# Gated DeltaNet decays: from triangle products on two engines to differences of running sums, in a two-layer decoder trunk

## The chip, the core and the metric

The kernel runs on one core of a Trainium2 chip. The core has TensorE (PE, with its weight loads PEld), VectorE (DVE), ScalarE (ACT), GpSimd (POOL) and SyncE (SP), which each work through their own instructions in order, and DMA engines that move data between DRAM and the core's memory. The metric is the device time of one execution in microseconds (us). Before the change the median of three runs is 2967.11 us, from 2965.97 to 2969.26.

## The reference

A trunk of two layers over 256 tokens of 2048 features: layer 0 mixes tokens by an mLSTM, layer 1 by a gated DeltaNet; both then attend to 256 memory tokens and apply a squared-ReLU MLP of 8192 features. All in float32. The change lies in the DeltaNet of layer 1 (32 value heads, 16 key heads, head size 128, chunks of 64). What matters of it:

```python
beta = jax.nn.sigmoid(bt)
g = -jnp.exp(a_log) * jax.nn.softplus(a + dt_bias)
gam = jnp.cumsum(to_chunks(g), axis=-1)
diff = gam[..., :, None] - gam[..., None, :]
A   = einsum('...id,...jd->...ij', kb, kc) * exp(where(strict, diff, -inf))   # kb = beta k
Aqk = einsum('...id,...jd->...ij', qc, kc) * exp(where(causal, diff, -inf))
# U, W by triangular solves with I + A; then a scan over the chunks
```

For each head and each pair of tokens j <= i the decay is the exponential of the sum of g over the tokens after j up to i.

## The kernel before, in words

Every product with weights streams units of one MB by SP's DMA queue into `raw`; ACT casts each half to `hi` (L88) and DVE makes the rest `lo` (L89), both rounded to float32r; PE multiplies hi by hi, hi by the input's lo and lo by hi. There are four raw halves and two hi and two lo tiles, so a unit is split while PE works on the one before it. In the DeltaNet's input product most units are tall: all 2048 rows and 128 columns, 48 matmuls of 256 columns, which give one block of 128 features of q (gq), k (gk), v (gv) or the gate (gz).

Each such block goes through `conv`: DVE scales it into a padded tile (`pad`), ACT multiplies it with the first tap (`cv`), DVE adds three taps, ACT applies Silu. POOL clears the pad's first columns.

The program treats all 256 tokens at once rather than chunks of 64: for each group of four value heads the function `pairs` builds blocks of A and of the query's matrix as [j, i] tiles of 128 by 128 tokens, for the token halves (0,0), (1,1) and (0,1). It asks `decays` for `dm` (the decay times beta), multiplies q and k by k on PE into the PSUM tiles g0 and g1 (g in the profile), scales and masks these into `gm` (DVE, and ACT for the third block), multiplies `gm` by `dm` into `at` (DVE, four instructions of 768 columns), and sends `at` to DRAM by POOL's queue (`at_d`, `a_d`), where a later stage reads it. PSUM tiles of the kind `ps` have three banks in turn for everything of that sort.

In `decays` before, POOL multiplies the triangle of ones (j <= i) by each head's g, once for the rounded part `gh` and once for the rest `gl` (L931). PE multiplies these by the opposite triangle, or by ones for the block (0,1), into `gep` (L935, six matmuls of 512 columns for a group), and ACT takes the exponential with ln beta as bias (L939), twelve instructions of 128 columns for a group. `norms` gives 1/norm of k (`rk`, by squares `l2sq` on ACT, sums `l` on PE, a square root on ACT and a reciprocal on DVE), which `gm` needs.

The order in the stage: for c = 0 to 3 four gq units, then `norms` and `pairs` of the group before, four gk units, then the other `pairs`; after c = 0 `gates` makes beta and g. Groups 6 and 7 lie among the first gv units. This is the program's order; the framework's scheduler sets the order on each engine from it, and interleaves neighbouring parts. The tables of ACT's functions are loaded where two neighbouring functions in its final order need different ones.

Of the kernel before, what the change touches and what calls it, by code (L numbers as in the profile page):

```python
# [7 lines left out]
F32 = mybir.dt.float32  # L8
# [6 lines left out]
P = 128  # L15
# [19 lines left out]
class Weights:  # L35
    """Streams weight units [128, kb, n] from DRAM and splits each into hi + lo."""
# [8 lines left out]
    def add(self, key, w, k0, kn, n0, nn, tall=False):  # L45
        """Units of 512 rows and 512 columns or, tall, of all the rows and 128 columns (64 at most: hi and lo side
        by side)."""
# [6 lines left out]
    def begin(self, place=None):  # L54
        """Starts the next unit's loads; returns the two halves' splits, to be called in order.
        place(j) gives other tiles to hold the unit: hi and lo of its j-th 128 rows."""
# [54 lines left out]
def trunk(ctx: ExitStack, tc, x, mem, norm_g, mem_norm_g, w_mem_kv, w_xq, w_xo, w_up, w_down,  # L111
# [56 lines left out]
    # rows j, columns i: j <= i, j < i, j > i  # L168
    tri_le, tri_lt, tri_gt = mask("tri_le", ALU.is_ge, 1), mask("tri_lt", ALU.is_gt, 1), mask("tri_gt", ALU.is_gt, -1)

    def behind(ins, *others):
        """Issue order on an engine: ins after each of the others."""
# [4 lines left out]
    # per-feature vectors as columns [128 features, 128-blocks]  # L177
# [27 lines left out]
    def feed(tok, c, h, gains, then=None):  # L205
        """Features 512 c .. of a token-major tile (t, 512 features): feature-major, gained and split into h."""
# [13 lines left out]
    class Rms:  # L220
        """Sums of squares along the features of token-major tiles [128 tokens, 512] by ACT."""
# [18 lines left out]
    def split_into(dst, src, scale=None):  # L240
        """dst[:, 0:256] = round(scale * src), dst[:, 256:512] = what is left."""
# [14 lines left out]
    def token_sums(parts, name):  # L256
        """Sums over the partitions of the parts' sum, as columns [128 tokens, 2]."""
# [11 lines left out]
    def spread(dst, col0, col1):  # L269
        """dst[p, t] = the token's scalar on every partition."""  # L270
        for t, c in enumerate((col0, col1)):
            PE.matmul(dst[:, t * P : (t + 1) * P], c.to_broadcast([P, P]), ident, start=True, stop=True)

    class Bank:
        """A block of a product: complete in the first 256 columns, or two parts in the two halves (wide)."""
# [4 lines left out]
    def extra_unit(u0):  # L280
        """Prepares one more unit of weights in tiles of u that are free around the end of a sub-layer."""
# [10 lines left out]
    def prod_feat(key, srcs, n_fb, evac, wide=True, before=None, fresh=False):  # L292
        """Feature-major product: srcs[k] = [128, hi 256 | lo 256]; evac(fb, bank).
        fresh: the sources are only being made, each one's hi first."""
# [30 lines left out]
    def prod_tall(key, srcs, n_fb, evac, before=None):  # L325
        """Feature-major product by tall units, one block after the other."""
# [921 lines left out]
```

## Time and profile before

| what | value |
|---|---|
| median of three runs | 2967.11 us |
| span of the profiled execution | 2962.9 us |
| PE busy in it | 2912.0 us (98%) |
| DVE, ACT, POOL busy | 1762.6, 1449.7, 137.1 us |
| mean granted PE clock | 0.996 |
| stage with the decays | 1313 to 1560 us, 247 us |
| PE, DVE, ACT, POOL busy in the stage | 233.6, 178.9, 154.1, 80.2 us |

The span runs from the first to the last instruction of the profiled execution; the time of that execution outside the span is not shown, and the median of the runs lies 4.2 us above it. The page names an engine's instructions by line, tile written and tiles read, with count, busy time and mean length, and with what its engine waited for just before. A wait belongs to whatever ended it last. PE's matmuls overlap, so a single duration is longer than the time a matmul adds to a full queue; the count in a stretch of full work gives the latter. Rows with a window give busy times in a stretch, in us from the span's start.

### The profile page before, as it was taken

The numbers are of one execution on the slowest core, as the hardware profiler recorded it, in microseconds if no ns is written. First come the engines' busy times: TensorE is split into PE (matmuls) and PEld (weight loads), VectorE is DVE, ScalarE is ACT, GpSimd is POOL, SyncE is SP. The second block draws the span as 40 slices with busy tenths as digits, with TensorE's granted clock in tenths as the row PEclk, the third lists the DMA queues.
The fourth block names the chain that finished last, engine by engine and source line by source line (L and its number), as shares of the span: only waits on it lengthen the run. The fifth ranks groups of instructions, "written<-read, shape, count | busy, mean of one in ns | idle before, by whom it ended". The sixth has DMA issues, their size and how long they took to land.

```text
span 2962.9 us, 43790 instructions
## 1 busy us (share of the span) xinstructions
PE 2912.0 (98%) x17363; PEld 2545.9 (86%) x17363; DVE 1762.6 (59%) x2560; ACT 1449.7 (49%) x2245; POOL 137.1 (5%) x256
## 2 busy tenths in 40 slices
PE   8999999999999999999999999999999999999998
PEld 7888888988888888898889998899888888888887
DVE  5555657644545555677779745445567546455565
ACT  6454546544434344566655444444456444344343
POOL 0000000000000000013231111000000000000000
PEclk9999999999999999999999999999999999999999
DMA  7545565555555565556778955665445565565554
GB/s 237 175 154 164 190 197 163 171 195 186 189 194 185 195 189 189 180 143 188 198 210 223 268 168 176 209 183 165 163 150 184 186 196 183 193 191 189 189 191 168
DMA packets 423120, 553.27 MB, mean 187 GB/s; under 512 B 22769, under 2 KB 220914, under 8 KB 420610
## 3 DMA queue, kind: packets, MB, share of 16 engines
q1 hardware_dynamic: 412608, 507.12, 55.5%
q0 software_dynamic: 8736, 42.02, 4.3%
q8 instruction: 136, 2.23, 0.3%
q10 hardware_dynamic: 1570, 1.33, 0.1%
q14 instruction: 70, 0.57, 0.1%
HBM read 527.29 MB, written 23.10 MB: 186 GB/s over the span
## 4 chain that ended last, share of the span: by engine, by line
PE 92%; DMA 3%; DVE 3%; ACT 2%; issue 1%; DVEq 0%; ACTq 0%; SPq 0%
PE up L314 15%; PE up L315 8%; PE down L378 8%; PE down L380 8%; PE down L379 8%; DMA raw<-in_gdn_w_in 3%; PE gz L334 2%; PE gz L335 2%; PE gz L333 2%; PE g_out L378 2%; PE g_out L379 2%; PE g_out L380 2%; PE o L314 2%; PE gv L333 1%; PE gv L334 1%; PE gv L335 1%
## 5 line engine op out<-in xcount | busy, mean ns | idle before, releaser
L89 DVE TENSOR_TENSOR lo<-raw,hi 128x1024 fp32r<-128x1024 f32 x938 | 1122.8, 1224 | 888.0 <-ACT hi L88 886.6
L88 ACT CAST hi<-raw 128x1024 fp32r<-128x1024 f32 x938 | 950.4, 1046 | 980.8 <-PE down L380 310.8
L314 PE MATMUL up<-h,hi 128*128 128x512 f32 x1920 | 678.7, 399 | 0.0
L315 PE MATMUL up<-h,lo 128*128 128x256 f32 x1920 | 539.2, 281 | 0.0
L314 PEld LDWEIGHTS up<-h,hi 128*128 128x128 f32 x1920 | 360.8, 188 | 89.9
L379 PE MATMUL down<-lo,u 128*128 128x512 f32 x1024 | 398.4, 389 | 0.0
L378 PE MATMUL down<-hi,u 128*128 128x512 f32 x1024 | 398.4, 389 | 0.0
L380 PE MATMUL down<-hi,u 128*128 128x512 f32 x1024 | 398.3, 389 | 0.0
L315 PEld LDWEIGHTS up<-h,lo 128*128 128x128 f32 x1920 | 362.7, 189 | 0.2
L380 PEld LDWEIGHTS down<-hi,u 128*128 128x128 f32 x1024 | 192.2, 188 | 40.0
L378 PEld LDWEIGHTS down<-hi,u 128*128 128x128 f32 x1024 | 192.2, 188 | 40.0
L379 PEld LDWEIGHTS down<-lo,u 128*128 128x128 f32 x1024 | 192.2, 188 | 39.7
L334 PE MATMUL gz<-h,hi 128*128 128x256 f32 x512 | 151.2, 295 | 0.0
L333 PE MATMUL gz<-h,hi 128*128 128x256 f32 x512 | 146.5, 286 | 2.5 <-ACT hi L88 2.5
L335 PE MATMUL gz<-h,lo 128*128 128x256 f32 x512 | 146.1, 285 | 0.8 <-DVE lo L89 0.8
L333 PE MATMUL gv<-h,hi 128*128 128x256 f32 x512 | 145.9, 285 | 0.5 <-ACT hi L88 0.5
L335 PE MATMUL gv<-h,lo 128*128 128x256 f32 x512 | 145.4, 284 | 0.0
L334 PE MATMUL gv<-h,hi 128*128 128x256 f32 x512 | 145.2, 284 | 0.0
L334 PEld LDWEIGHTS gz<-h,hi 128*128 128x128 f32 x512 | 97.8, 191 | 6.2 <-issue 6.2
L378 PE MATMUL g_out<-hi,u 128*128 128x512 f32 x256 | 100.9, 394 | 0.0
L379 PE MATMUL g_out<-lo,u 128*128 128x512 f32 x256 | 100.7, 393 | 0.0
L333 PEld LDWEIGHTS gz<-h,hi 128*128 128x128 f32 x512 | 97.9, 191 | 3.1 <-ACT hi L88 2.7
(415 smaller groups left out, 4889.0 us busy)
## 6 DMA issues: line engine op xcount, KB each, us to landing
raw<-in_w_up SPq DMA_DIRECT2D x256, 512.0 KB, 3.9
raw<-in_w_down SPq DMA_DIRECT2D x256, 512.0 KB, 4.0
raw<-in_gdn_w_in SPq DMA_DIRECT2D x192, 512.0 KB, 5.0
raw<-in_mlstm_w_in SPq DMA_DIRECT2D x96, 512.0 KB, 4.0
raw<-in_gdn_w_out SPq DMA_DIRECT2D x64, 512.0 KB, 4.4
raw<-in_mlstm_w_out SPq DMA_DIRECT2D x32, 512.0 KB, 4.5
at_d<-at POOLq DMA_DIRECT2D x8, 1536.0 KB, 7.6
ab<-at_d POOLq DMA_DIRECT2D x8, 1536.0 KB, 7.6
```

The lines of the kernel that those rows point to most:

```text
L88: a = nc.scalar.copy(h_, raw[:, :, :n])
L89: return a, nc.vector.tensor_tensor(l_, raw[:, :, :n], h_, ALU.subtract)
L314: PE.matmul(a[:fw], wh, srcs[kk][:, :], start=(kk == 0), stop=False, skip_group_check=True)
L315: PE.matmul(a[:fw, T:], wl, srcs[kk][:, 0:T], start=False, stop=(kk == nk - 1), skip_group_check=True)
L333: PE.matmul(a[:, 0:T], hi[k], srcs[k][:, 0:T], start=(k == 0), stop=False)
L334: PE.matmul(a[:, 0:T], hi[k], srcs[k][:, T:], start=False, stop=False)
L335: m = PE.matmul(a[:, 0:T], lo[k], srcs[k][:, 0:T], start=False, stop=(k == nk - 1))
L378: PE.matmul(accs[t], sh, hi[j], start=(kk == 0), stop=False)
L379: PE.matmul(accs[t], sh, lo[j], start=False, stop=False)
L380: PE.matmul(accs[t], sl, hi[j], start=False, stop=(kk == nk - 1))
```

## The change

`gates` makes the running sums of g within each half of 128 tokens instead of the two rounded parts: `cum` as columns (a token for each partition, a head for each column) and, by the same product the other way round, `cumr` as rows (a head for each partition). The rows go to DRAM (`g_d`). `load_rows` reads four heads' rows back by POOL's queue, the same 512 values to every partition (`grow`), two loads for a group; groups 0 and 1 are loaded after `gates`, each further one at the end of `decays` two groups ahead. `decays` subtracts the column's value as a scalar from the row and limits the difference to at most zero (`gdiff`, DVE, two buffers that share the tag of the norms' gains), and ACT takes the exponential with the same biases as before. The block (0,1) needs no difference: its bias is the sum over the rest of the first half, so ACT reads `grow` itself. There are 96 exponentials as before. Neither `gep` nor POOL's products remain. Comments were also removed, and line numbers shift by 1 to 14.

```diff
@@ gates
-                gh = sc.tile([P, 2, 32], F32R, name="gh")
-                V.tensor_copy(gh, g)
-                gl = sc.tile([P, 2, 32], F32R, name="gl")
-                V.tensor_tensor(gl, g, gh, ALU.subtract)
                 p_ = psum("suf")
                 PE.matmul(p_[:, 0:32], tri_gt, g[:, 0, :], start=True, stop=True)
+                for t in range(2):
+                    PE.matmul(p_[:, 32 + t * 32 : 64 + t * 32], tri_le, g[:, t, :], start=True, stop=True)
+                    PE.matmul(p_[0:32, P + t * P : 2 * P + t * P], g[:, t, :], tri_le, start=True, stop=True)
                 sufb = sc.tile([P, 32], F32, name="sufb")
                 V.tensor_tensor(sufb, p_[:, 0:32], lnb[:, 0, :], ALU.add)
-                return lnb, gh, gl, sufb
+                cum = sc.tile([P, 2, 32], F32, name="cum")
+                V.tensor_copy(cum, p_[:, 32:96].rearrange("p (t h) -> p t h", t=2))
+                cumr = sc.tile([32, 2 * P], F32, name="cumr")
+                V.tensor_copy(cumr, p_[0:32, P : 3 * P])
+                nc.gpsimd.dma_start(g_d, cumr)
+                return lnb, cum, sufb
+
+            rows_of = {}
+
+            def load_rows(grp):
+                rows_of[grp] = []
+                for tt in range(2):
+                    r_ = acts.tile([P, 4, P], F32, tag=f"u{8 + grp % 2 * 2 + tt}", name="grow")
+                    src = g_d[grp * 4 : grp * 4 + 4, tt * P : (tt + 1) * P]
+                    nc.gpsimd.dma_start(r_, src.unsqueeze(0).to_broadcast([P, 4, P]))
+                    rows_of[grp].append(r_)
 
             def decays(grp):
                 dm = [acts.tile([P, 2, 3, P], F32, tag=f"y{grp % 2 * 2 + i}", name="gdm") for i in range(2)]
-                for blk, tt, lhs in ((0, 0, tri_gt_r), (1, 1, tri_gt_r), (2, 1, ones_r)):
-                    ep = psum("gep")
-                    if blk < 2:
-                        rr = []
-                        for i, src in enumerate((gh, gl)):
-                            r_ = acts.tile([P, 4, P], F32R, tag=f"u{8 + 2 * tt + i}", name=f"gl{tt}{i}")
-                            G.tensor_tensor(r_, tri_le[:, None, :].to_broadcast([P, 4, P]),
-                                            src[:, tt, grp * 4 : grp * 4 + 4].unsqueeze(2).to_broadcast([P, 4, P]), ALU.mult)
-                            rr.append(r_)
-                    for i in range(2):
-                        PE.matmul(ep, lhs, rr[i].rearrange("p h i -> p (h i)"), start=(i == 0), stop=(i == 1))
-                    for hh in range(4):
-                        hv = grp * 4 + hh
-                        b_ = sufb[:, hv : hv + 1] if blk == 2 else lnb[:, tt, hv : hv + 1]
-                        S.activation(dm[hh // 2][:, hh % 2, blk, :], ep[:, hh * P : (hh + 1) * P], AF.Exp, bias=b_)
+                gr = rows_of.pop(grp)
+                for hh in range(4):
+                    hv = grp * 4 + hh
+                    d = tmp.tile([P, 2, P], F32, tag="gain", name="gdiff")
+                    for tt in range(2):
+                        V.tensor_scalar(d[:, tt, :], gr[tt][:, hh, :], cum[:, tt, hv : hv + 1], 0.0,
+                                        ALU.subtract, ALU.min)
+                    o_ = dm[hh // 2][:, hh % 2]
+                    for tt in range(2):
+                        S.activation(o_[:, tt, :], d[:, tt, :], AF.Exp, bias=lnb[:, tt, hv : hv + 1])
+                    S.activation(o_[:, 2, :], gr[1][:, hh, :], AF.Exp, bias=sufb[:, hv : hv + 1])
+                if grp + 2 < GV_H // 4:
+                    load_rows(grp + 2)
                 return dm
@@ the loop over c
-                    lnb, gh, gl, sufb = gates()
+                    lnb, cum, sufb = gates()
+                    load_rows(0)
+                    load_rows(1)
```

The scheduler gives other orders on three engines. First ACT, in the gq units of c = 2 (rows are line, instruction, tile written and tile read; hi is a cast, cv a convolution's first tap, gqk its Silu). Before:

```order
L88 CAST hi_11815<-raw_0_11817 128x1024
L88 CAST hi_11815<-raw_8_11819 128x1024
L868 ACTIVATE cv<-pad,cols 128x256
L88 CAST hi_11883<-raw_0_11885 128x1024
L871 ACTIVATE gqk_11743<-cv 128x256
L868 ACTIVATE cv<-pad,cols 128x256
L88 CAST hi_11883<-raw_8_11887 128x1024
L871 ACTIVATE gqk_11744<-cv 128x256
```

And in the change, at the same place:

```order
L88 CAST hi_11891<-raw_0_11893 128x1024
L88 CAST hi_11891<-raw_8_11895 128x1024
L948 ACT_TABLE_LOAD
L948 ACTIVATE gdm<-gdiff,lnb 128x128
L872 ACT_TABLE_LOAD
L872 ACTIVATE gqk_11752<-cv 128x256
L869 ACTIVATE cv<-pad,cols 128x256
L88 CAST hi_11959<-raw_0_11961 128x1024
L88 CAST hi_11959<-raw_8_11963 128x1024
```

One exponential of a later group now stands between the cast and the Silu, with a table load on either side; before, a group's exponentials stood together.

Second PE, at the first pairs: in the change the end of the first gk unit of c = 1 (gk_11425) and what follows; g_11395 and g_11396 are of group 0, the other g of group 1, gk_11493 the next unit.

```order
L335 MATMUL gk_11425<-h_10290,lo_11254 128x256
L993 MATMUL g_11395<-gqk_10425 128x512
L994 MATMUL g_11396<-gqk_10425 128x256
L993 MATMUL g_11719<-gqk_10426 128x512
L994 MATMUL g_11720<-gqk_10426 128x256
L993 MATMUL g_11731<-gqk_10427 128x512
L333 MATMUL gk_11493<-h_10275,hi_11415 128x256
L334 MATMUL gk_11493<-h_10275,hi_11415 128x256
L333 MATMUL gk_11561<-h_10275,hi_11483 128x256
L334 MATMUL gk_11561<-h_10275,hi_11483 128x256
L335 MATMUL gk_11493<-h_10275,lo_11416 128x256
```

Before, the next unit followed the first at once, with gep and g singly among its matmuls; now five g stand in a row ahead of it.

Third DVE, at the end of group 3, before the weights `lo_12462` of the unit gq_12539, the second gq unit of c = 3 (gk_12335 is the last gk unit of c = 2, gq_12471 the first gq unit of c = 3). Before:

```order
L992 TENSOR_TENSOR at<-gm,gdm 128x6x128
L870 SCALAR_TENSOR_TENSOR cv<-pad,cols,cv 128x256
L984 SCALAR_TENSOR_TENSOR gm<-g_12431,rk,tri_lt 128x128
L986 SCALAR_TENSOR_TENSOR gm<-g_12432,rk,tri_lt 128x128
L984 SCALAR_TENSOR_TENSOR gm<-g_12431,rk,tri_le 128x128
L986 SCALAR_TENSOR_TENSOR gm<-g_12432,rk,tri_le 128x128
L89 TENSOR_TENSOR lo_12456<-raw_8_12459,hi_12455 128x1024
L992 TENSOR_TENSOR at<-gm,gdm 128x6x128 x2
L865 TENSOR_TENSOR pad<-gq_12465,rb 128x256
L89 TENSOR_TENSOR lo_12524<-raw_0_12525,hi_12523 128x1024
```

And in the change:

```order
L998 SCALAR_TENSOR_TENSOR gm<-g_12438,rk,tri_lt 128x128
L871 SCALAR_TENSOR_TENSOR cv<-pad,cols,cv 128x256
L998 SCALAR_TENSOR_TENSOR gm<-g_12438,rk,tri_le 128x128
L871 SCALAR_TENSOR_TENSOR cv<-pad,cols,cv 128x256 x2
L944 TENSOR_SCALAR gdiff<-grow,cum 128x128 x4
L1004 TENSOR_TENSOR at<-gm,gdm 128x6x128 x4
L89 TENSOR_TENSOR lo_12462<-raw_0_12463,hi_12461 128x1024
L89 TENSOR_TENSOR lo_12462<-raw_8_12465,hi_12461 128x1024
```

The four at stood in smaller pieces with a lo among them; now they stand together, ahead of both halves of the lo.

More of the change, by code (lines that the diff above doesn't have):

```diff
@@ L855, in gdn @@
         v_d = tc.dram_tile([GV_H // 4, P, 2, 512], F32, name="v_d")
+        g_d = tc.dram_tile([32, 2 * P], F32, name="g_d")
         rs = Scales(rms.rstd, "gd")
@@ L889, in gdn @@
         with tc.tile_pool(name="gd1", bufs=1) as sc:
-            tri_gt_r = sc.tile([P, P], F32R, name="tri_gt_r")
-            V.tensor_copy(tri_gt_r, tri_gt)
-            ones_r = sc.tile([P, P], F32R, name="ones_r")
-            V.tensor_copy(ones_r, ones)
             dtb = sc.tile([P, 32], F32, name="dtb")
```

## The prediction

> **What bounds the kernel now.** I read the page's busy shares and its chain first, then the tables by stretch for the stage that the change touches, then what TensorE (PE) waits for there.
>
> ```profile
> span 2962.9 us, 43790 instructions
> PE 2912.0 (98%) x17363; PEld 2545.9 (86%) x17363; DVE 1762.6 (59%) x2560; ACT 1449.7 (49%) x2245; POOL 137.1 (5%) x256
> PE 92%; DMA 3%; DVE 3%; ACT 2%; issue 1%; DVEq 0%; ACTq 0%; SPq 0%
> ```
>
> PE is busy 98% of the span and holds 92% of the chain, so a matmul taken away is worth its slot, unless PE then waits. The runs' median is 2967.11, 4.2 us above this span; I make the sum on the span and carry the 4.2.
>
> ```profile
> core 0: us, PE busy (x) PEld busy (x) DVE busy (x) ACT busy (x) POOL busy (x), PEclk, DMA share, GB/s
> 1160.00:1180.00 20.00, 20.00 (x90) 16.57 (x89) 11.94 (x12) 9.06 (x13) 0.00 (x0) 1.00 0.60 197
> 1240.00:1260.00 20.00, 20.00 (x171) 20.00 (x170) 15.03 (x25) 14.74 (x31) 0.00 (x0) 1.00 0.53 142
> 1320.00:1340.00 20.00, 17.45 (x112) 14.20 (x111) 12.86 (x21) 16.46 (x36) 10.05 (x11) 1.00 0.18 59
> ...
> 1377.00:1441.00 64.00, 60.84 (x446) 56.45 (x445) 45.78 (x75) 39.28 (x70) 20.14 (x34) 0.97 0.67 184
> ...
> 1313.00:1560.00 247.00, 233.62 (x1735) 216.66 (x1734) 178.94 (x295) 154.09 (x276) 80.21 (x138) 0.99 0.69 190
> ```
>
> The last row is the stage with the decays: 247 us, in which PE sits idle 13.4. The first two rows give the slots of a full PE, which the single durations (400 and 283 ns, overlapping) do not: 20/90 = 0.222 us for a matmul of 512 columns, 20/171 = 0.117 for one of 256. A weight unit of 48 is thus 5.6 us. The row 1377 to 1441 is one c, four gq and four gk units: PE 60.8 us, ACT 39.3.
>
> ```profile
> PE gk L335 <- DVE lo L89: 5.2, 6, 1.2
> ...
> PEld gk L335 <- DVE lo L89: 9.0, 6, 2.0
> ```
>
> In that stage PE waits mostly for weights not yet split (lo by VectorE, DVE, after hi by ScalarE, ACT). So whatever delays a hi or lo there is paid by PE.
>
> **What goes.** 48 matmuls on gep, and their operands made by POOL.
>
> ```profile
> L935 PE MATMUL gep<-gl,tri_gt_r x32: 387/397/589, 1315.4 to 1522.5; 128*128 128x512 f32 x32
> ...
> L935 PE MATMUL gep<-gl,ones_r x16: 392/410/500, 1324.9 to 1523.0; 128*128 128x512 f32 x16
> ...
> L334 PE MATMUL gk<-h,hi 128*128 128x256 f32 x192 | 56.6, 295 | 0.0
> ...
> L334 PE MATMUL gq<-h,hi 128*128 128x256 f32 x190 | 53.7, 283 | 0.0
> ```
>
> 48 x 0.222 = **-10.7 us**, all on PE (bounds -10 and -13, from two gep taking 0.27 us apart at worst). The gk units, which carry the pairs, run 295 ns a matmul, gq units 283: 576 gk matmuls x 12 ns = 6.9 us. Part of it is restarts after waits and a lower clock, the rest the gep between them and their late operands; I take **-6** (0 to -7), since whole waits are counted as idle time and not here.
>
> ```profile
> 1304.90 0.48 DVE L870 SCALAR_TENSOR_TENSOR cv<-pad,cols,cv 128x256 f32<-128x256 f32 x1
> 1305.68 1.27 DVE L870 SCALAR_TENSOR_TENSOR cv<-pad,cols,cv 128x256 f32<-128x256 f32 x1
> ...
> 1305.64 1.04 POOL L931 TENSOR_TENSOR gl<-tri_le,gh 128x512 fp32r<-128x512 f32 x1 [7.03 <-DVE sufb L919]
> ```
>
> The same DVE instruction takes 0.48 us, and 1.27 when POOL's multiplication runs beside it: DVE is slowed while POOL multiplies.
>
> ```profile
> L89 DVE TENSOR_TENSOR lo<-raw,hi 128x1024 fp32r<-128x1024 f32 x938 | 1122.8, 1224 | 888.0 <-ACT hi L88 886.6
> ...
> L89 DVE TENSOR_TENSOR lo<-raw,hi 128x1024 fp32r<-128x1024 f32 x69 | 89.7, 1306 | 31.7 <-ACT hi L88 31.7
> ...
> L992 DVE TENSOR_TENSOR at<-gm,gdm 128x768 f32<-128x768 f32 x32 | 34.6, 1111 | 0.5
> ...
> L992 DVE TENSOR_TENSOR at<-gm,gdm x32: 950/954/1793, 1329.0 to 1548.5; 128x768 f32<-128x768 f32 x32
> ...
> 1295.95 0.22 DVE L836 TENSOR_SCALAR sp_u<-sp_e 128x128 f32<-128x128 f32 x1
> ```
>
> On DVE 64 differences come in, of the same form as L836: 64 x 0.22 = 14 us. The POOL multiplications go: lo (mean 1306 ns here, 1224 on the whole page) and at (mean 1111, median 954) give back 69 x 0.08 + 32 x 0.16 = 10.7. DVE's sum rises by some 3 us in 247, of which it works 179: nothing on PE by itself; what counts is where the pieces stand.
>
> **What comes: the start.** Four small matmuls more in gates, before the first pairs.
>
> ```profile
> 1305.03 0.38 PE L917 MATMUL suf<-g,tri_gt 128*128 128x32 f32 x2 [0.58 <-DVE g L911]
> ...
> rk_d<-rkt POOLq DMA_DIRECT2D x2, 16.0 KB, 3.0
> ...
> ti<-t_d POOLq DMA_DIRECT2D x16, 128.0 KB, 5.0
> ```
>
> The one there takes 0.38; four more **+1.0** (0.4 to 1.5). The rows of g's sums then go to DRAM and back: sufb is made at 1305.4 now; with cum, cumr and a lo ahead of them the store leaves about 1307.4, lands 3.0 later (as rk_d), and the first load, 512 pieces like ti, 5 to 6 after that: 1316. The first gdiff stands in DVE's queue before pad of the last gq block, and DVE comes to it at about 1312.5, so DVE waits 3 to 4 us, and conv of that block with it. The next lo in DVE's queue is far behind, and the weights of the next unit are split already: 0 on PE, inside the 6.7 below. Later loads are issued two groups (over 30 us) ahead. Their transfer: 0.53 of the DMA time moved 142 GB/s in pieces of 512 bytes (row 1240), 268 GB/s when busy, so 256 KB take 1.0 us and all 16 loads 16 us, DMA share 0.69 to 0.75: hidden.
>
> **What comes: ACT's order.** The Exp are as many (96), but each now waits only for its own difference, and the scheduler has set them singly between the Silu of the convolutions. Exp and Silu need different tables.
>
> ```profile
> 1506.71 1.13 ACT L960 ACTIVATE l2sq<-gqk 128x512 f32<-128x512 f32 x2
> 1507.86 1.28 ACT L939 ACT_TABLE_LOAD   x1
> 1509.16 0.37 ACT L939 ACTIVATE gdm<-gep,lnb 128x128 f32<-128x128 f32 x1
> 1509.54 1.28 ACT L871 ACT_TABLE_LOAD   x1
> 1510.84 0.42 ACT L871 ACTIVATE vT<-cv 128x256 f32<-128x256 f32 x1
> 1511.27 1.28 ACT L266 ACT_TABLE_LOAD   x1
> 1512.57 0.27 ACT L266 ACTIVATE rk<-l,eps_t 128x8 f32<-128x8 f32 x1
> 1512.85 1.28 ACT L939 ACT_TABLE_LOAD   x1
> 1514.15 1.91 ACT L939 ACTIVATE gdm<-gep,lnb 128x128 f32<-128x128 f32 x7
> ```
>
> A load takes 1.28 us; in a row an Exp takes 1.91/7 = 0.27. ACT's order has 51 table loads before and 92 now: 41 x 1.28 = 52.6 us more. Per c there were 5; now 13, 16 and 17, so ACT's 39.3 us become 49.6, 53.4 and 54.7, against PE's 60.8 less 2.7 of gep. On average ACT stays just below PE: no cost from the sum. [...]
>
> ```profile
> 1326.88 0.86 PE g L981 x2
> ...
> 1329.62 0.43 PE g L982 x2
> ...
> L88 ACT CAST hi<-raw 128x1024 fp32r<-128x1024 f32 x70 | 72.0, 1042 | 42.7 <-DMA raw<-in_gdn_w_in 32.7 <-PE gv L334 4.3 <-PE gk L334 3.2
> ...
> L868 ACT ACTIVATE cv<-pad,cols 128x256 f32<-128x256 f32 x34 | 17.2, 506 | 4.9 <-DVE pad L865 4.9
> ...
> L988 ACT ACTIVATE gm<-g,rk 128x256 f32<-128x256 f32 x16 | 7.5, 471 | 8.3 <-DVE gm L984 8.3
> ```
>
> A unit all but fits too: two casts of 1.04, cv and Silu 0.5 and 0.4, and load, Exp, load 2.9 are 5.9 us against PE's 5.6, with weights one unit ahead. Two kinds of place do not.
>
> (a) First pairs. PE has five g products in a row (three of L981 at 0.86, two of L982 at 0.43: 3.4 us) before gk_11493, whose hi ACT casts only after rk, a load, ten Exp and two gm, and whose lo DVE splits after four at. From rk, about 0.6 after the end of gk_11425: load 1.3, Exp 2.7, gm 0.5, at 4 x 0.95 = 3.8, lo 1.2: 9.5. Wait 0.6 + 9.5 - 3.4 = **6.7**; now this place idles 2.6 (row 1320). The sixth group, with its three g in a row, has the same shape at about half: **3.5**. (b) The ends of groups 3, 5 and 7: all four at stand before the lo of the unit after next. In group 3, ACT has after its last cast two sets of load, Exp, load, Silu (3.4 each, with one Exp run of three), cv and gm: 8.2; then at and lo 5.0. PE has about 1.7 of gk_12335 left, g 1.7 and gq_12471 5.6: 9.0. Wait **4.2**, three times 12.6. Together 22.8 against today's 13.4: **+9.4** (bounds: -8, if ACT and DVE come early and only 5 are left; +25, if each new load pair adds a us).
>
> Sum: -10.7 - 6 + 1.0 + 9.4 = **-6.3**, span 2956.6, time **2960.8**.
>
> **Rivals.** One is **that the waits shrink**: DVE free of POOL, gep out of PE's queue and PSUM's three banks with less in turn. Waits fall to about 5: -10.7 - 6 + 1 - 8.4 = -24, 2943; waits that stay at today's 13.4 give -15.7, 2951. For it: DVE's 1.27 for 0.48. Against: four at ahead of a lo. Another is **hidden anyway**: the stage is paced by the chain l2sq, rk, gm, at, lo, not by PE's count; the saved slots become longer waits, 2967 plus 1 for gates: 2968. For it: today's 13.4 us of waits are nearly all of that chain.
>
> The **slower** one: ACT becomes the bound of each unit. Its point: a cast that starts more than 5.6 - 1.04 - 1.22 = 3.4 us after PE began the unit before. A unit with load, Exp, load has 5.9 us on ACT; if the Silu in it also waits for DVE's three taps (3 x 0.48 = 1.4), 7.3 against 5.6, 1.7 over. With 20 such pairs 34 us: 2995 from the forecast's sum; with half of them covered, 2978. For it: 13 to 17 loads per c; against: 5 us of ACT are free per c by the sum.
>
> Last, **a switch costs twice its load**: were another 1.28 behind each of the 41, ACT's 154 + 105 = 259 us pass the stage's 247 by 12, and with its waits for DVE on top the time is some 2995. [...]
>
> **Numbers.** About 0.2% (5.9 us) is what a measurement here can tell from no change. Forecast (2951 to 2970) 0.47, of which 0.26 is faster by over 0.2%, 0.19 within, 0.02 slower, since it stands at the edge; waits shrink 0.16, faster; hidden 0.14, within but for 0.01; ACT the bound 0.21, slower; doubled switch 0.02, slower. Faster 0.42, within 0.32, slower 0.26. The range 2945 to 2981 leaves out the far ends of the shrinking waits and half of ACT's case, some 0.18. Its sides are the bounds above: -16 and +20 about the forecast, less than all of them at once.
>
> **What would show it.** No L935 and no POOL multiplication; ACT with 41 more loads of 1.28, and 50 to 55 us busy per c; PE's idle time in the stage near 23 us; lo waits after the four at of groups 3, 5 and 7 near 4 us; the first gdiff waiting for grow at about 1316. Wrong would be: a PE wait that ends on ACT hi in most units (ACT the bound), on grow after the first group (DMA), or a stage shorter than 235 us (waits shrank). If the stage from the first l to the last g product is about 241 us, the forecast holds by its own steps.

## The result, and the profile after

The changed kernel takes 2975.51 us in the median of seven runs (2974.22 to 2979.06), the kernel before 2967.99 beside it (2965.97 to 2969.26). The ratio is 1.0027 [1.0017, 1.0038] (in brackets, here and below, the 95% interval): slower by 7.5 us, where 2960.8 was forecast. First the page of the kernel after.

```profile
span 2973.2 us, 43804 instructions
PE 2911.2 (98%) x17323; PEld 2546.4 (86%) x17323; DVE 1763.4 (59%) x2622; ACT 1507.1 (51%) x2286; POOL 109.9 (4%) x241
PE 90%; DMA 4%; ACT 3%; DVE 2%; issue 1%; DVEq 0%; POOL 0%; ACTq 0%; SPq 0%; POOLq 0%
```

PE works 0.8 us less than before in a span that is 10.3 us longer. 48 matmuls have gone (10.7 us by the prediction's slots), and PE's busy time did not fall: so other matmuls took longer. Where, the table by stretch of the kernel after shows (the columns are those of the prediction's tables; the last but two is the granted clock).

```profile
1313.00:1560.00 247.00, 223.69 (x1642) 208.84 (x1642) 179.63 (x354) 208.67 (x315) 55.86 (x121) 0.96 0.73 201
...
1320.00:1324.00 4.00, 1.06 (x10) 0.86 (x9) 1.79 (x6) 2.49 (x6) 0.00 (x0) 1.00 0.55 153
1324.00:1331.00 7.00, 7.00 (x35) 7.00 (x35) 0.96 (x3) 6.90 (x10) 0.10 (x1) 0.51 0.00 0
...
1377.00:1441.00 64.00, 60.44 (x464) 57.74 (x463) 51.14 (x97) 58.61 (x88) 14.96 (x34) 0.97 0.87 234
1420.00:1426.00 6.00, 3.41 (x25) 2.79 (x23) 4.39 (x6) 5.99 (x9) 0.51 (x1) 1.00 0.05 12
1426.00:1430.00 4.00, 3.69 (x18) 3.69 (x19) 4.00 (x6) 3.97 (x10) 3.85 (x8) 0.57 1.01 341
1540.00:1545.00 5.00, 1.98 (x16) 1.72 (x14) 4.51 (x12) 4.94 (x8) 0.10 (x1) 1.00 1.02 307
1545.00:1549.00 4.00, 3.85 (x22) 3.88 (x23) 1.46 (x4) 3.94 (x6) 0.10 (x1) 0.62 0.49 130
```

PE sits idle 23.3 us in the stage (247.0 less 223.69; before 13.4). ACT's busy time there went from 154 to 209 us. And the granted clock is 0.96 instead of 0.99: at the three places shown PE waits 2.6 to 3.0 us, in one piece or several, and for 3.4 or 6.8 us behind them every matmul runs at half the clock, 35 of them in 7 us where a full PE, at the 0.117 us of the prediction's row 1240, does 60.

To see all of it, the span of each kernel is cut into three parts: PE's idle time (span less busy PE); what the clock takes from busy PE (for each row of one us of the whole span the busy share times one less the granted clock; the 7 us row above gives 7 x 0.49 = 3.4); and the rest, which is PE's work at the full clock.

| profiled execution | span | idle PE | clock's loss | rest |
|---|---|---|---|---|
| before | 2962.9 | 50.9 | 10.0 | 2902.0 |
| after | 2973.2 | 62.0 | 18.4 | 2892.8 |
| difference | +10.3 | +11.1 | +8.4 | -9.2 |
| of it between 1300 and 1580 us | | +9.9 | +6.5 | |

The work did get shorter by what gep and gates were worth. The waits and the clock took back about twice that. The two executions are not equally typical, though: in every run that has both figures the time lies 1.7 to 2.1 us above the span, so the median of the kernel before, 2967.99, stands for a span of some 2966, and about 3 of the 10.3 us come from which executions were profiled. Over the recorded runs of that kernel the span goes from 2955.4 to 2972.5 us as the granted clock goes from 0.998 to 0.992, so these 3 us are most likely part of the clock's 8.4.

The waits of PE after, 1300 to 1590 us (total, times, longest; l sums the squares l2sq, bq is a small scale that DVE makes from l, vp transposes v):

```profile
PE l L976 <- ACT l2sq L972: 5.2, 3, 2.9
PE gv L333 <- ACT hi L88: 3.9, 3, 1.8
PE vp L885 <- DVE gm L998: 3.2, 1, 3.2
PE g L993 <- DVE bq L981: 2.2, 3, 0.8
PE g L993 <- DVE gm L998: 2.0, 2, 1.2
PE gq L333 <- ACT hi L88: 1.9, 2, 1.4
PE gk L333 <- ACT hi L88: 1.8, 1, 1.8
PE gk L335 <- DVE lo L89: 0.9, 2, 0.6
```

Before, 5.2 us of the stage's waits ended on lo, from DVE. Now 2.2 do (0.9 at gk, the rest at gv and gq); some 13 end on ACT, on a cast or a square that stands in ACT's queue behind other work.

### The profile page after: what moved, and what is told of

It reads as the page before. It is cut to its first block, busy times and chain, and to the rows that moved or that the text cites. A ratio compares the mean times of both kernels' runs of the same rounds, so it can differ in the third digit from the quotient of the medians.

```text
span 2973.2 us, 43804 instructions
## 1 busy us (share of the span) xinstructions
PE 2911.2 (98%) x17323; PEld 2546.4 (86%) x17323; DVE 1763.4 (59%) x2622; ACT 1507.1 (51%) x2286; POOL 109.9 (4%) x241
## 4 chain that ended last, share of the span: by engine, by line
PE 90%; DMA 4%; ACT 3%; DVE 2%; issue 1%; DVEq 0%; POOL 0%; ACTq 0%; SPq 0%; POOLq 0%
PE up L314 15%; PE up L315 8%; PE down L379 8%; PE down L378 8%; PE down L380 8%; DMA raw<-in_gdn_w_in 2%; PE gz L334 2%; PE gz L335 2%; PE gz L333 2%; PE o L314 2%; PE g_out L378 2%; PE g_out L379 2%; PE g_out L380 2%; PE gv L333 1%; PE gv L334 1%; PE gv L335 1%
## 5 line engine op out<-in xcount | busy, mean ns | idle before, releaser
L333 PEld LDWEIGHTS gv<-h,hi 128*128 128x128 f32 x512 | 100.2, 196 | 5.7 <-ACT hi L88 5.5
L871 DVE SCALAR_TENSOR_TENSOR cv<-pad,cols,cv 128x256 f32<-128x256 f32 x192 | 91.8, 482 | 20.6 <-ACT cv L869 19.2
```

The lines of the kernel that those rows point to most:

```text
L333: PE.matmul(a[:, 0:T], hi[k], srcs[k][:, 0:T], start=(k == 0), stop=False)
L871: V.scalar_tensor_tensor(c, pad[:, j : j + T], w[j], c, ALU.mult, ALU.add)
```

## The experiments

Kernels that share a heading ran on one chip and share the runs of the kernel before.

### Fewer loads, more loads, no rows: four kernels beside 2965.64

The **batch** kernel is the change with ln beta folded into the difference. DVE writes the exponent straight into dm, for the block (0,1) too, and one Exp does two heads.

```diff
+                lc = sc.tile([P, 2, 32], F32, name="lc")
+                V.tensor_tensor(lc, lnb, cum, ALU.subtract)
...
+                        for tt in range(2):
+                            V.tensor_scalar(o_[:, tt, :], gr[tt][:, hh, :], lc[:, tt, hv : hv + 1],
+                                            lnb[:, tt, hv : hv + 1], ALU.add, ALU.min)
+                        V.tensor_scalar(o_[:, 2, :], gr[1][:, hh, :], sufb[:, hv : hv + 1], None, ALU.add)
+                    S.activation(dm[i], dm[i], AF.Exp)
```

> The change with ln beta folded into the difference on DVE (row + (ln beta - cum), at most ln beta) and the block (0,1)'s bias added there too, so that ACT takes one exponential for two heads: 16 of them in place of 96, and 53 table loads in place of 92. DVE has 32 more small instructions. Theory loads (the 41 table loads between casts and Silu make ACT late with hi): 2957 to 2962, faster than the kernel before. Rival start (the rows' way over DRAM delays the first group, and this is the loss): 2972 to 2976, as the change. Rival DVE (what DVE has more, in front of lo, is the loss): 2976 to 2982.

Measured: 2956.86, ratio 0.9963 [0.9949, 0.9977]. It beats both kernels, by as much as the theory of the loads had it. It changes more than the loads, though: ACT takes 16 exponentials in place of 96, and DVE does 32 operations more.

The **group** kernel leaves the operations as they are, gives the differences four buffers and holds each exponential of a group behind the group's last difference.

```diff
-                    d = tmp.tile([P, 2, P], F32, tag="gain", name="gdiff")
+                    d = sc.tile([P, 2, P], F32, tag="gdiff", bufs=4, name="gdiff")
...
+                        x_ = S.activation(o_[:, tt, :], d[:, tt, :], AF.Exp, bias=lnb[:, tt, hv : hv + 1])
+                        behind(x_, v)
```

> The change with four difference tiles and each group's exponentials held, in ACT's order, behind the last difference of their group; 71 table loads in place of 92. Theory loads: about half of the loss comes back, 2965 to 2970. Rival start: 2973 to 2977. Rival DVE: 2973 to 2977.

Measured: 2975.27, ratio 1.0031 [1.002, 1.0043], a miss of the theory and inside both rivals' range. The order still sets exponentials singly between Silus, only later: at 1425 to 1434 us five loads stand between one cast and the next, and PE's longest wait for hi becomes 6.0 us. Holding the exponentials back does not keep them together.

The **switch** kernel is the kernel before with an exponential of one column ahead of 21 of the stage's Silus, 34 loads more (a0 is the convolution's first tap, s_ its Silu; `behind` sets the order of issue).

```diff
+            if ch in EXTRA:
+                e_ = S.activation(warm, ones[:, 0:1], AF.Exp)
+                behind(e_, a0)
+                behind(s_, e_)
```

> The kernel before, with gep and all, and one exponential of a single column put ahead of the Silu of 21 convolutions in the stage (its result is not used): 85 table loads in place of 51. Theory loads: slower than before by the change's loss and what it saved on PE, 2980 to 2990. Rivals start and DVE: 2968 to 2971, since ACT has room for 34 x 1.28 = 44 us.

Measured: 2972.37, ratio 1.0022 [1.0013, 1.0031], span 2967.4. 34 loads cost 6.7 us against the shared 2965.64 (3.9 to 9.2 by the interval), between the theory's 14 to 24 and the rivals' 2 to 5. They are 43.6 us of ACT's time (34 x 1.28); most of it is covered, a sixth is paid. By the three parts, in the quickest of its eleven runs, PE is idle 6.0 us more and the clock takes 3.2 less: its waits are many and short, the longest 1.9.

The **nodma** kernel is the change without the rows' way through DRAM. Its rows are constants, so the decays are not the reference's; the instructions on DVE and ACT stay.

```diff
+            for r_ in grow_:
+                G.memset(r_, -0.5)
...
             def load_rows(grp):
+                rows_of[grp] = grow_[grp % 2 * 2 : grp % 2 * 2 + 2]
```

> The change with the rows set to a constant once instead of loaded by DMA (the decays are not those of the reference): nothing waits for rows; 94 table loads. Theory loads: 2972 to 2976, as the change, since the loads stay. Rival start: 2964 to 2968. Rival DVE: 2973 to 2976.

Measured: 2969.17, ratio 1.0011 [1.0002, 1.002]. It gives back some 4 to 6 us of the change's 7.5, though it has two loads more; the time lies between the ranges of the two theories. In its trace PE has no wait from 1304 to 1324 us. So the rows' lateness, which the prediction put at "0 on PE", is a cost. How it reaches PE is seen in the kernel after itself, in the timeline of the stage's start (start, length, what; in brackets the idle time before it and what ended that):

```profile
1318.42 0.28 DVE L944 TENSOR_SCALAR gdiff<-grow,cum 128x128 f32<-128x128 f32 x1 [4.25 <-DMA grow<-g_d]
...
1318.74 0.40 ACT L948 ACTIVATE gdm<-gdiff,lnb 128x128 f32<-128x128 f32 x1 [5.10 <-DVE gdiff L944]
...
1321.50 0.48 DVE L944 TENSOR_SCALAR gdiff<-grow,cum 128x128 f32<-128x128 f32 x2 [2.20 <-DMA grow<-g_d]
1321.90 0.42 DVE L866 TENSOR_TENSOR pad<-gq,rb 128x256 f32<-128x256 f32 x1
1322.35 0.51 ACT L869 ACTIVATE cv<-pad,cols 128x256 f32<-128x256 f32 x1 [1.48 <-DVE pad L866]
1322.76 1.13 ACT L972 ACTIVATE l2sq<-gqk 128x512 f32<-128x512 f32 x2
...
1323.43 0.72 PE L976 MATMUL l<-ones,l2sq 128*128 128x2 f32 x5 [2.94 <-ACT l2sq L972]
```

The second load lands at 1321.5. Behind its difference on DVE stands pad, behind pad's cv on ACT stands l2sq, and PE, in order, waits 2.94 us for a square that has nothing to do with the rows. The same wait stands in batch (5.4 us) and, further down, in silu (4.7), whose rows are late too; best has none, and early and early_silu, with rows in time too, have 0.5 and 1.1.

### Rows in time, no loads, no decays: four kernels beside 2966.36

The **early** kernel puts the gates' weights and the gates ahead of the first four gk units.

```diff
-                prod_k(c)
                 if c == 0:
                     lnb, cum, sufb = gates()
                     load_rows(0)
                     load_rows(1)
-                else:
+                prod_k(c)
+                if c:
                     pairs(c * 2 - 1)
...
```

> The change with the gates' unit of weights and the gates themselves ahead of the first four gk units instead of behind them, so that the running sums go to DRAM and back some 22 us before the first difference needs them. The order then holds 104 table loads, 12 more than the change. Theory rows late: in the change PE sits idle 2.9 us at 1320.5 for l2sq, which stands in ACT's queue behind an exponential whose difference waits for the rows until 1318.4, and PE's granted clock is 0.5 for 6.8 us right after it. Both go: -2.9 and some -2.7, 2970 (2968 to 2972). Theory loads (the table loads set the pace): 12 more at the 0.19 us a load that the 34 extra loads cost in the kernel before, +2.3: 2976 to 2979. Rival order (the at of a group stand together ahead of a lo, whatever comes before): 2974 to 2977.

Measured: 2994.02, ratio 1.01 [1.0084, 1.0116], outside all three ranges. The rows come in time and the scheduler, with more exponentials ready early, strews more of them. One place, ACT first, then PE:

```profile
1491.15 1.03 ACT L88 CAST hi<-raw 128x1024 fp32r<-128x1024 f32 x1
1492.20 1.28 ACT L948 ACT_TABLE_LOAD   x1
1493.50 0.70 ACT L948 ACTIVATE gdm<-gdiff,lnb 128x128 f32<-128x128 f32 x2
1494.21 1.28 ACT L872 ACT_TABLE_LOAD   x1
1495.51 0.42 ACT L872 ACTIVATE gqk<-cv 128x256 f32<-128x256 f32 x1
...
1496.34 1.28 ACT L948 ACT_TABLE_LOAD   x1
1497.64 0.40 ACT L948 ACTIVATE gdm<-gdiff,lnb 128x128 f32<-128x128 f32 x1
1498.06 1.28 ACT L872 ACT_TABLE_LOAD   x1
...
1502.38 1.98 ACT L88 CAST hi<-raw 128x1024 fp32r<-128x1024 f32 x2
...
1503.47 0.58 PE L333 MATMUL gv<-h,hi 128*128 128x256 f32 x1 [6.62 <-ACT hi L88]
```

Ten us lie between the end of one cast and the start of the next, with five loads in them (four are shown), and PE waits 6.62. This is the prediction's slower rival, ACT as the bound of a unit, in full: a cast that comes too late because of the loads ahead of it. Not in each unit, though: two places, at 1360 and 1496 us, hold 15 of the 36 us that PE is idle in this stage.

The **silu** kernel is the change with Silu in place of Exp for the decays, so that no load is needed among them.

```diff
-                        S.activation(o_[:, tt, :], d[:, tt, :], AF.Exp, bias=lnb[:, tt, hv : hv + 1])
+                        S.activation(o_[:, tt, :], d[:, tt, :], AF.Silu, bias=lnb[:, tt, hv : hv + 1])
...
```

> The change with Silu in place of Exp in the 96 activations of the decays, which leaves the decays wrong but the instructions as many and as large; no table load stands among them, 39 in all instead of 92. Theory loads: 53 loads fewer at 0.19 us (34 extra loads in the kernel before cost 6.5 us): -10, 2965 (2963 to 2968). If every load were paid by PE: -53 x 1.28 = -68. Rival order: the at stand together ahead of a lo as before, and the rows are as late; -0 to -3, 2972 to 2976.

Measured: 2961.22, ratio 0.9982 [0.997, 0.9994]: 14.3 us less than the change, or 12.7 when each is taken against its own runs of the kernel before; the theory had 10, and 2963 to 2968. The order of ACT's work is another one without the loads too, so these 13 to 14 us are for the loads and the order that goes with them; the two were not taken apart.

The **best** kernel is batch with early's order (both diffs above).

> The batch kernel (ln beta folded into the differences, one exponential for two heads) with the gates ahead of the first gk units as well; 59 table loads. Theory rows late: the batch kernel has 4.7 us of idle PE at 1317 to 1323 and 10.2 us at half the clock behind it; both go, -4.7 and -4: 2948 to 2951. If the rows' lateness only takes the place of a wait of the pairs that would come anyway: 2955 to 2958, as the batch kernel.

Measured: 2945.75, ratio 0.9937 [0.992, 0.9955], better than expected and far ahead of both kernels. PE's idle time between 1300 and 1580 us is 4.1 us, from 13.9 in batch, and these are its waits there:

```profile
PE l L978 <- ACT l2sq L974: 1.9, 3, 0.7
PE vp L885 <- ACT v L887: 0.9, 1, 0.9
PE vp L885 <- DVE gm L1000: 0.9, 1, 0.9
```

The **floor** kernel is the kernel before without decays: dm is set to one, once.

```diff
+            for d_ in dm_all:
+                G.memset(d_, 1.0)
+
+            def decays(grp):
+                return dm_all[grp % 2 * 2 : grp % 2 * 2 + 2]
```

> The kernel before with the decays left out: dm is set to one once by POOL; no products on POOL, no gep, no exponentials of the decays, 39 table loads. What any way of making the decays can gain at most. My sum's gep term with its pace term: -10.7 - 6 and nothing for waits, against 2967: 2950. If the pace term is nothing: 2956. If the waits for the decays go too, as the rival of shrinking waits had it (-8.4): 2942 to 2948.

Measured: 2940.92, ratio 0.9923 [0.9906, 0.994]. The time lies just under the lowest of the three ranges; the decays cost 25.4 us in the kernel before. Its rest is 2886.8, 15.2 less than before, its clock's loss in the stage 0.0 and its idle time there 4.6, so the waits went too. The best kernel, with decays, comes within 5 us of it.

### The table of two by two, and the price of a wait: four kernels beside 2966.84, two beside 2965.49

The **early_silu** kernel is early with Silu for the decays, the fourth corner.

> The early kernel (gates ahead of the first four gk units) with Silu in place of Exp in the activations of the decays, so again without a table load among them (40 in all) and with wrong decays. With the change (2975.5), early (2994.0) and silu (2961.2) it makes a table of two by two. Theory loads and rows together: without loads nothing is lost by the rows coming in time, and what the rows' lateness cost comes back: PE sat idle 4.7 us at 1317 in the silu kernel with 10.2 us at half the clock behind it, -4.7 and -5: 2951 (2948 to 2954). Rival: in the early kernel it is the order itself that costs (exponentials of a group strewn over the units, the differences ahead of a lo), not the loads in it: 2975 to 2990.

Measured: 2947.62, ratio 0.9932 [0.9915, 0.9949].

| | rows late | rows in time |
|---|---|---|
| loads strewn | 2975.5 (the change) | 2994.0 (early) |
| no loads among the decays | 2961.2 (silu) | 2947.6 (early_silu) |
| batch's exponentials, 53 and 59 loads in all | 2956.9 (batch) | 2945.8 (best) |

The two causes do not add. Without strewn loads, rows in time are worth 11 to 14 us; in early, with them, 18 to 20 are lost. (The kernels stand within 2.5 us of one another by their runs of the kernel before; the ranges are with and without that.) PE's idle time from 1300 to 1580 us says the same: 23.9 in the change, 36.1 in early, 17.3 in silu, 9.2 in early_silu, against 14.0 before.

The loss in early is not the price of rows in time as such: nodma has its rows in time and 94 loads, and gained 4 to 6 us. What costs in early is the order that came with the gates' new place, 104 loads in all, with five between two casts; why that order and not nodma's came out so much worse was not taken apart.

The **gates_first** kernel, a control, has the kernel before with its gates in the early place.

> The kernel before with the gates' unit and the gates ahead of the first gk units: a control for the best kernel, whose gain over the batch kernel is put down to the rows of the running sums coming in time. The kernel before has no such rows, so nothing is to be gained: 2964 to 2969. If the place of the gates gains by itself (their chain of small operations away from the first pairs): 2957 to 2960.

Measured: 2964.08, ratio 0.9991 [0.9982, 1.0001]: at most 5.3 us, and by the interval perhaps nothing, come from the place of the gates alone.

The kernels with **gaps** measure what a wait of PE costs. They are the kernel before, and in the second layer's up product, after 2266 us, the first half's cast to hi is repeated in some units (u counts the product's units).

```diff
+                ups = [j for j, (key_, _) in enumerate(self.plan) if key_ == "up"]
+                u = i - ups[len(ups) // 2]
+                if i in ups and 0 <= u and u % 5 == 2 and k0 == 0:
+                    for _ in range(7):
+                        nc.scalar.copy(h_, raw[:, :, :n])
```

That is gap_long. In gap_short it is `u % 3 != 2` and five copies, in gap_1 the same with four, in gap_half every unit with three and one of half the size.

> The kernel before, with the first half's cast to hi made eight times over in 13 of the units of the second layer's up product, far from the stage, so that PE waits there for about 8 x 1.05 - 5.6 = 2.8 us each time and works at its full pace between: 36 us of idle PE in all. Theory clock (a wait of some 3 us lowers the granted clock to a half for the 3.4 us behind it or twice that, at a loss of 1.7 or 3.4 us): some 7 to 13 stretches at half the clock, +36 and +12 to +25, 3015 to 3028. If a wait costs only itself: 3003.

> As the kernel with the long waits, but with six casts in place of one in 43 units, two of every three, so that PE waits some 0.7 us each time (6 x 1.05 - 5.6): 30 us of idle PE in short pieces. Theory clock: short waits leave the clock as it is; the time rises by the idle sum alone, and the clock lost in the span stays within 5 us of the 11.0 of the kernel before. If the clock falls by the share of idle time, however cut: as much lost per us of wait as with the long ones.

> As the kernel with the short waits, with five casts in place of one in two of every three units of the second layer's up product. One cast less than there, where the waits were mostly 2.0 to 2.7 us: waits of 1.0 to 1.6 us, some 43 of them, 50 us of idle PE. Theory clock, as the stage's rows have it so far (every wait over 3 us was followed by a stretch at half the clock, of those from 0.5 to 1.5 us about a quarter): about 10 stretches, 17 us of clock lost, 0.3 us for each us of idle. If the clock falls by the share of idle time, however cut: 0.45 us for each, 23.

> As above with four casts and one of half the size in place of one, in every unit of the second layer's up product: waits of 0.3 to 1.0 us, some 60 of them, 20 to 50 us of idle PE. Theory clock: short waits leave the clock as it is, less than 5 us lost in the up product, however many they are. If the clock falls by the share of idle time: 0.45 us for each us of idle, 9 to 23.

Measured, from 2266 us to the end, where the kernel before loses nothing to the clock (waits and clock from one profiled execution each; gap_1 and gap_half ran twice, gap_1 with 3025.4 and 3036.7):

| kernel | time | waits, us in total | clock's loss there | per us of wait |
|---|---|---|---|---|
| gap_half | 3008.85 | 32, 16.5 | 3.0 | 0.18 |
| gap_1 | 3031.08 | 37, 38.6 | 6.6 | 0.17 |
| gap_short | 3095.98 | 37, 76.8 | 33.6 | 0.44 |
| gap_long | 3058.84 | 16, 64.3 | 29.0 | 0.45 |

The times themselves missed: the waits came out longer in gap_long and gap_short, where ACT's queue holds the product's own copies among the casts, than 8 x 1.05 - 5.6 has it. In gap_half some 20 us of the slowdown are in none of the sums: its rest is that much over the kernel before, and where they come from was not shown. What the runs tell is the clock. gap_short came out as its rival had it, with as much lost per us as in gap_long, but its waits, 2.1 us in the mean, are not the short ones that were meant. gap_1 lost less than either of its forecasts, 0.17 per us of wait for 0.3 and 0.45; gap_half is inside its theory's 5 us. PE's waits of gap_half:

```profile
PE up L320 <- ACT hi L94: 9.3, 18, 0.8
PE up L321 <- DVE lo L95: 3.9, 13, 0.3
PE up L324 <- ACT hi L94: 3.4, 1, 3.4
```

All of its clock's loss stands behind the one wait of 3.4 us, at the product's start; none stands behind the 31 short ones. And one of the long waits of gap_long, by stretch:

```profile
2321.00:2325.20 4.20, 0.00 (x0) 0.00 (x0) 2.15 (x6) 4.20 (x8) 0.00 (x0) 0.73 0.04 14
2325.20:2328.70 3.50, 3.42 (x9) 2.41 (x10) 3.48 (x5) 2.50 (x4) 0.00 (x0) 0.50 0.30 66
2328.70:2332.00 3.30, 3.30 (x18) 2.93 (x17) 0.69 (x1) 0.00 (x0) 0.00 (x0) 0.84 0.86 286
```

In the traces with waits in the stage or in the up product, each of 29 waits of 3 us or more had a stretch at half the clock that began in it or within 3.6 us of its end; of 28 waits of 1.5 to 3 us in gap_short and gap_1, 16 had one; of 43 of 0.3 to 1.5 us in the up product of gap_1 and gap_half, one (waits that fell into such a stretch are not counted). So the loss does not go by the share of idle time in the whole product. But in the stage of all the traces 37 of 176 waits of 0.3 to 1.5 us had a stretch behind them: there several come close together. The length of a single wait is thus not the whole rule either; the last section has what the traces show in its place.

## Why the prediction was wrong, step by step

The time lies inside the range of 2945 to 2981, but on the slower side of the kernel before, where a gain was forecast. On the span the forecast missed 16.6 us, 2973.2 for 2956.6. By the terms of its sum 6 of them are the pace, which was not there, 8.4 the clock, which had no term (some 3 of these may be the choice of executions), 1.7 the waits and 0.5 what goes. The waits came out near their number by luck: two steps that made them, "no cost from the sum" for ACT's loads and "0 on PE" for the rows, were wrong, and the waits that were forecast came out smaller.

**What goes: right in the main, the pace wrong.** gep at -10.7 and gates at +1.0 make -9.7; the rest fell by 9.2. The **-6** for the pace of the gk units was not there. The rows of the gk units in the stage after:

```profile
L333 PE MATMUL gk<-h,hi 128*128 128x256 f32 x192 | 56.8, 296 | 1.8 <-ACT hi L88 1.8
L335 PE MATMUL gk<-h,lo 128*128 128x256 f32 x192 | 56.5, 295 | 0.9 <-DVE lo L89 0.9
L334 PE MATMUL gk<-h,hi 128*128 128x256 f32 x192 | 55.4, 288 | 0.0
```

They mean 293 ns, with no gep among them, where the row in the prediction had 295: the 12 ns over 283 come mostly from elsewhere, here from matmuls at half the clock (up to 681 ns). In the other kernels without gep the rest fell by 10 to 14 us, in floor by 15, so a pace term of 0 to some -4 is what can be said. The prediction's bounds of 0 to -7 held it; the value was taken from the wrong end, after the sentence that named "restarts after waits and a lower clock" as a part.

**The clock: a term that was missing.** The sum held PE's waits at their own length. In the traces each of the 97 windows of 3.4 us at full clock with 2 us of idle PE or more has behind it a stretch of 3.4 us at half the clock, which costs 1.7 us, and at 1324 in the kernel after there are two in a row. In the stage five places paid, at 1324 (6.8 us at half the clock), 1426, 1511, 1546 and 1556 (3.4 each), against two before: 9.9 us and 3.4. Of the forecast's error this is 6.5 us, 8.4 over the whole span. That the clock falls at all stood in the prediction, as the 0.97 in the row 1377 to 1441; what it hangs on did not, since the two stretches of the stage before, at 1381 and 1446, stand behind waits of only 0.6 and 1.2 us.

**The start: "0 on PE", measured 2.9 and its clock.** The first difference ran at 1318.4 (1316 was forecast), DVE waited 4.25 and then 2.20 (3 to 4), conv waited with it, and so far the step was right. It then looked for the next lo behind the wait and found none near. It did not look for what else PE would wait for: l2sq, behind cv, behind pad. The wait went through two queues in order and came to PE on another tile.

**ACT's loads: "no cost from the sum", measured 13 to 14 with their order.** That ACT's sum stays below PE's was true by a hair in the row asked for: 58.61 us busy in 1377 to 1441, PE 60.44; 49.6 to 54.7 were forecast. But an average under the bound pays nothing only if the pieces come evenly, and the prediction itself had shown, with DVE's four at, that they do not. The order had 41 loads more, and the trace has them at the length the prediction used:

```profile
L872 ACT ACT_TABLE_LOAD x30 | 38.5, 1283 | 0.5
L948 ACT ACT_TABLE_LOAD x26 | 33.4, 1283 | 0.4
```

The 0.5 and 0.4 us are all the idle time ahead of these 56 loads, and in the timeline the instruction behind a load starts 0.01 to 0.02 us after its end, but for three that wait for DVE (5.1, 2.0 and 0.2 us). So the rival of a doubled switch falls.

**The waits: the right sum of wrong parts.** Idle PE in the stage was forecast at 22.8 us and measured at 23.3, by luck. By places it is this (some 1.6 us in three short waits are left out):

| place | forecast | measured | ended by |
|---|---|---|---|
| start, 1320 | 0 | 2.9 | l2sq |
| first pairs, 1332 to 1342 | 6.7 | 4.4 | bq, gm, hi, lo |
| sixth group, 1509 to 1523 | 3.5 | 2.8 | l2sq, bq, gm |
| end of group 3, 1422 to 1426 | 4.2 | 2.9 | hi, hi, l2sq |
| end of group 5, 1484 to 1489 | 4.2 | 3.1 | gm, hi, lo |
| end of group 7, 1551 to 1557 | 4.2 | 2.3 | gm, hi, hi |
| vp, 1542 to 1545 | 0 | 3.2 | gm |

The four at do stand ahead of a lo at groups 3, 5 and 7, and PE does wait at each of these places. But the waits end mostly on hi, not on lo: ACT is later than DVE. The wait at vp, 1.8 us in the kernel before and 3.0 in nodma, was not followed to its start. And early_silu, with rows in time and no loads, leaves 9.2 us of idle PE between 1300 and 1580, where the kernel before has 14.0. By that, DVE's order alone would not have cost the forecast's +9.4; the first rival's reasons (DVE free of POOL, gep out of the queue) were sound, and the loads and the late rows took their gain back. That early_silu's order differs from the change's elsewhere too is the limit of this argument.

**The relief of DVE: right.** In the stage's rows after, at takes 953 ns (before 1111) and lo 1220 (before 1295 in the same stretch): DVE works 179.6 us there against 178.9.

**The rivals.** ACT as the bound of each unit was to give 2978 to 2995 and stood at 0.21; the time, 2975.5, lies just below, by its mechanism at some units and the rows' lateness at the start. "Hidden anyway" had 2968 and is out. The forecast's yardstick, about 241 us from the first l to the last g, was no use: it is 226 us before and 225 after, since g stands elsewhere among the units now. The start of the solver's first multiplication tells it better: 1574.2 us before, 1582.4 after.

The sum as it came out, against the span: gep and gates -9.2 with no pace, idle PE +11.1, clock +8.4, together +10.3; forecast were -15.7, +9.4 and 0.

## What to carry to other kernels

Price the idle time of the matmul engine by how much of it falls together. The 31 short waits of gap_half, each alone and 0.8 us at the longest, had no stretch at half the clock behind them; 2 us or more within a window of 3.4 us, in one piece or in several, had one in all 97 cases here, so here they cost their own length and 1.7 us on top, or 3.4 where two followed. When work on an engine becomes ready piece by piece instead of all at once, ask where a scheduler will set the pieces and what each setting costs; here one large exponential for two heads, with the bias moved into DVE's instruction, was worth 16 to 19 us, and moving the gates ahead so that the rows come in time helped only where the loads were not strewn. A late transfer must be followed through every queue in order behind the instruction that waits for it, until it comes to the engine that sets the end; here DVE's 2.20 us for grow came through pad, cv and l2sq to PE as 2.94.

## What the runs showed of the hardware

In the traces the granted clock falls from 1.00 to 0.50 and to nothing between, for 3.4 us (at 1426 in the kernel after) or two or three times that (6.8 at 1324 there, 10.2 in batch and silu). Its changes keep to a grid: in each of the sixteen traces all of them lie a whole number of 3.4133 us apart, to within 0.01 us; in the kernel after, for instance, at 1324.11, 1330.93, 1426.51 and 1429.92, and the last, at 2965.92, lies 736 such steps behind the first, at 453.71. Cut along this grid, that kernel's trace reads:

```profile
1320.69:1324.11 3.42, 0.68 (x6) 0.69 (x7) 1.90 (x6) 1.93 (x5) 0.00 (x0) 1.00 0.42 114
1324.11:1327.52 3.41, 3.41 (x18) 3.41 (x18) 0.85 (x3) 3.35 (x5) 0.10 (x1) 0.50 0.00 0
...
1423.10:1426.51 3.41, 1.05 (x6) 0.64 (x6) 3.41 (x5) 3.41 (x5) 1.02 (x2) 1.00 0.01 2
1426.51:1429.92 3.41, 3.41 (x17) 3.41 (x17) 3.41 (x4) 3.38 (x8) 3.33 (x7) 0.50 1.13 389
1481.12:1484.53 3.41, 2.74 (x22) 2.46 (x21) 1.29 (x4) 3.38 (x7) 0.00 (x0) 1.00 0.08 18
1484.53:1487.95 3.42, 1.64 (x8) 0.97 (x6) 3.42 (x5) 3.42 (x5) 0.02 (x1) 1.00 0.00 0
1487.95:1491.36 3.41, 2.72 (x23) 2.54 (x22) 3.41 (x5) 3.41 (x10) 3.41 (x7) 1.00 0.75 288
```

PE is idle 2.7 us in the first window and 2.4 us, in pieces, in the one that ends at 1426.51, and the window behind each is at half the clock; the 3.1 us in pieces at 1483 are split over three windows, 0.7, 1.8 and 0.7, and nothing follows. Over the sixteen traces, after their first 10 us, all 97 windows at full clock with 2 us of idle PE or more were followed by one at half the clock, 47 of 160 with 1.2 to 2 us, and 15 of 322 with 0.3 to 1.2 us; those 15, two of them in the kernel before, and 3 of some 13,000 with less are not explained here. So a wait's loss hangs on where the grid lies, which differs from trace to trace (its first change is at 453.71 us in the kernel after and at 453.01 in the kernel before), and a short wait can pay when others stand close to it.

34 more table loads, 43.6 us of ACT, cost 6.7 us when they were spread among short work, and 53 fewer, with the order that goes with them, gained 13 to 14. In these two pairs a sixth and a fifth of the loads' time were thus paid, the order included; five loads between two casts, 6.4 us of ACT, came with a wait of PE of 6.6 us.
